# One decoder layer on one core: three strands' products issued later, a division moved from VectorE to ScalarE, and x loaded ahead of the first weights

## The chip, the cores and the metric

The kernel runs on one core of a Trainium2 chip. The metric is the device time of one execution in microseconds (us). TensorE is called PE, VectorE DVE, ScalarE ACT, GpSimd POOL; SP is SyncE, which here only issues DMAs. PEld is the loading of weights into TensorE.

## The reference, cut to what matters

One layer over 256 tokens of width 1024, batch 1, in float32: a token mixer, a mixture of 32 experts, and a per-layer embedding, each followed by a layer norm.

```
proj = h @ w_in                       # 1024 x 10768: operands of all branches and three gates
y_a = gdn_branch(...) @ w_o_gdn       # gated delta rule, chunks, 8 heads of 128
y_b = lru_branch(...) @ w_o_lru       # conv, gated linear recurrence, GeLU gate
y_c = swa_branch(...) @ w_o_swa       # window attention, softmax with a sink
mix = (g_a * y_a + g_b * y_b + g_c * y_c) @ w_out
x = layer_norm(2**0.25 * x + mix)
x = layer_norm(2**0.25 * x + moe(x))  # top 4 of 32: x @ w_gu[e], SwiGLU, @ w_down[e]
x = layer_norm(2**0.25 * x + sigmoid(x Wg) * (p Wp))
```

Two details matter here. The delta rule needs `g = -exp(a_log) * softplus(a + dt_bias)`, its running sum, and the inverse of a triangular 64x64 matrix per head and chunk. The attention needs `probs = pexp / (sum(pexp) + exp(sink - m))`.

## The kernel before, in words

The program has two parts. `mixer` (to about 453 us of the profiled execution) does the token mixer and the router; `moe` then streams 12 MB of weights for each of the 32 experts.

In `mixer`, PE's work is a list of units. A column unit is 24 products of 128x256 (L367), a wide unit 12 products of 128x512 (L377). Each unit needs one 512 KB piece of weights. `load` (L416) has SP fetch it into one of four buffers `w`; `split` casts it on ACT into a high part HI (L423) and subtracts on DVE (L426) and POOL (L428) into a low part LO; HI and LO have three places each, and a piece is split two units ahead of its use. `rows_by` and `column` then multiply high by high, high by low and low by high.

Beside the units run strands: Python generators that `run` steps once a unit, after the unit's products are issued. A `yield` in a strand puts what follows behind the next unit's products on every engine. So the number of yields between an operation and the product that reads it sets how much other PE work lies between them. Each engine takes its instructions in the order in which they were issued and waits for each in turn. Strands that the change touches:

- `softplus` (L278 to L296): a chain of small DVE operations. `parameters` uses it for the recurrence, `evac_ab` for the decay g. After it `evac_ab` multiplies by -exp(a_log) (L597), yields, and has PE form the running sums (L600 to L602); after another yield ACT copies them out (L604) and the event "G" is set.
- `decays` waits for "G" and then has PE spread the sums over 128 columns (L671), four times.
- `inverse` writes its 16x16 blocks to DRAM and back in another layout (L751, L756), yields twice, transposes on DVE (L760) and then runs bursts of 32x32 products on PE: L765 (64 of them), L774 and L777 (64 each).
- `attend`, four times: scores and maximum (L1000 to L1013), exponentials with their sums on ACT (L1017, L1018), sum and reciprocal on DVE (L1022, L1023), the division as a multiplication on DVE (L1025, L1026, eight operations), transposes on PE (L1041), the product with the values (L1053).
- `bias_parts` loads b_gu in twelve pieces of 64 KB through POOL's DMA queue (L234) and splits each into three parts on ACT and POOL (L240, L242, L244).

At the start SP issues the first piece of w_in, then x in four pieces, then more weights; ACT and DVE split the first piece, PE turns x (L271), and units begin.

In `moe` SP loads the experts' weights into ten buffers of 2 MB in a ring; a load waits until PE has done with the buffer.

Of the kernel before, what the change touches and what calls it, by code (L numbers as in the profile page):

```python
# [14 lines left out]
ALU = mybir.AluOpType  # L15
# [5 lines left out]
P = 128  # L21
# [90 lines left out]
def mixer(mx, tc, nc, a, xs, rt, dram, cst, ones, el):  # L112
# [38 lines left out]
    def bank(i):  # L151
        return lambda: pg.tile([P, 512], F32, name="pg", tag=f"pg{i}", bufs=1)
# [25 lines left out]
    def wait(*names):  # L178
        while not all(n in events for n in names):
            yield  # L180
# [10 lines left out]


    warm = mp.tile([P, 1], F32, name="warm")
    pool.memset(warm, 0.0)
    act.dma_start(cst[:, 0:P], a["cst"][:, 0:P])
    act.activation(warm, warm, AF.Sigmoid)
# [28 lines left out]
    def bias_parts():  # L225
        yield from wait("late", "lru")
        raw_b = mp.tile([96, 512], F32, name="rawb")
        bsrc = a["b_gu"][0].rearrange("(g e) (q c) -> g (e q) c", g=4, q=4)
        dve.tensor_add(rt.pick, ident[:96, 0:32], ident[:96, 32:64])
        dve.tensor_add(rt.pick, rt.pick, ident[:96, 64:96])  # L230
        yield
        for g_ in range(4):
            for n in range(3):
                pool.dma_start(raw_b[32 * n:32 * n + 32], bsrc[g_])  # L234
            yield
            yield
            v = rt.bias[:, g_]
            for whole, rows in ((slice(0, 96), (slice(0, 96),)), (slice(64, 96), (slice(32, 64), slice(64, 96)))):
                for r in rows:
                    act.copy(v[r], raw_b[r])  # L240
                yield
                pool.tensor_tensor(out=raw_b[whole], in0=raw_b[whole], in1=v[whole], op=ALU.subtract)  # L242
                yield
            act.copy(v[64:96], raw_b[64:96])  # L244

    pool.memset(ones, 1.0)
    mhalf = mpa.tile([P, 16], F32, name="mhalf")
    pool.memset(mhalf, -0.5)
    upper = mpa.tile([P, 1], F32, name="upper")
# [26 lines left out]
    def softplus(dst, src, n, neg):  # L276

        e = m2.tile([P, n], F32, name="spe", tag="spe")  # L278
        s = m2.tile([P, n], F32, name="sps", tag="sps")
        q = m2.tile([P, n], F32, name="spq", tag="spq")  # L280
        act.activation(e, src, AF.Abs)
        act.activation(e, e, AF.Exp, scale=-1.0)
        yield
        dve.tensor_scalar(s, e, 2.0, None, op0=ALU.add)
        dve.reciprocal(s, s)
        dve.tensor_mul(s, s, e)
        dve.tensor_mul(q, s, s)
        dve.tensor_scalar(e, q, 1.0 / 17, None, op0=ALU.mult)
        yield
        for c in (15, 13, 11, 9, 7, 5, 3):  # L290
            dve.scalar_tensor_tensor(e, e, 1.0 / c, q, ALU.add, ALU.mult)
            if c in (13, 9, 5):
                yield
        dve.scalar_tensor_tensor(e, e, 1.0, s, ALU.add, ALU.mult)
        dve.tensor_scalar(q, src, -1.0 if neg else 1.0, 0.0, op0=ALU.mult, op1=ALU.max)
        dve.scalar_tensor_tensor(dst, e, 2.0, q, ALU.mult, ALU.add)  # L296
# [114 lines left out]
    def load(n):  # L411
        if n < len(order):
            i = order[n][0]
            raw[i] = wp.tile([P, KD * P], F32, name="w", tag="w")
            src = pieces[i][0]
            sync.dma_start(raw[i].rearrange("p (k c) -> p k c", k=src.shape[1]), src)  # L416
# [161 lines left out]
    def evac_ab(ps):  # L578
        abr = m2.tile([16, T], F32, name="abr", tag="sq")
        act.copy(abr, ps[:16])  # L580
        yield
        p2 = yield from banks.take()
        for t in range(2):
            pe.transpose(p2[:, t * 16:(t + 1) * 16], abr[:, t * P:(t + 1) * P], ident[:16, :16])
        yield
        act.copy(ab, p2[:, :32].rearrange("p (t c) -> p t c", t=2))
        banks.done(p2)
        for t in range(2):
            dve.tensor_add(kd[:, t], ab[:, t, 0:H], dtb)
            act.activation(beta[:, t], ab[:, t, H:16], AF.Tanh, scale=0.5)  # L590
        yield
        dve.tensor_scalar(beta, beta, 0.5, 0.5, op0=ALU.mult, op1=ALU.add)
        yield from softplus(flat(g), flat(kd), 16, False)
        act.activation(alog, alog, AF.Exp)
        yield
        for t in range(2):
            dve.scalar_tensor_tensor(g[:, t], g[:, t], -1.0, alog, ALU.mult, ALU.mult)  # L597
        yield
        p2 = yield from banks.take()
        pe.matmul(p2[:, 0:16], cen, flat(g), start=True, stop=True)  # L600
        pe.matmul(p2[:, 16:24], highh, g[:, 0], start=True, stop=True)
        pe.matmul(p2[:, 24:32], lowh, g[:, 1], start=True, stop=True)  # L602
        yield
        act.copy(gcc, p2[:, :32])  # L604
        banks.done(p2)
        dve.tensor_scalar(nG, Gf, -1.0, None, op0=ALU.mult)
        dve.tensor_add(eG[:, 1], Gf[:, 1], c1)
        dve.tensor_sub(eG[:, 0], gl0, Gf[:, 0])
        dve.tensor_add(eq, Gf[:, 1], c1)
        act.activation(eG, eG, AF.Exp)  # L610
        act.activation(eq, eq, AF.Exp)
        events.add("G")
# [46 lines left out]
    def decays():  # L659

        yield from wait("G")
        dts = []
        for t in range(2):
            dt_ = yield from probs.take()
            dts.append(dt_)
            d8 = dt_.rearrange("p a c -> p (a c)")[:, :8 * P].rearrange("p (h c) -> p h c", h=8)
            for h4 in range(2):
                ps = yield from banks.take()
                for i in range(4):
                    h = 4 * h4 + i  # L670
                    pe.matmul(ps[:, i * P:(i + 1) * P], Gf[:, t, h:h + 1].to_broadcast([P, P]), ident, start=True, stop=True)  # L671
                yield
                for i in range(4):
                    h = 4 * h4 + i
                    dve.scalar_tensor_tensor(d8[:, h], ps[:, i * P:(i + 1) * P], nG[:, t, h:h + 1], cmask, ALU.add, ALU.add)
                banks.done(ps)
                yield
                act.activation(d8[:, 4 * h4:4 * h4 + 4], d8[:, 4 * h4:4 * h4 + 4], AF.Exp)
        yield from wait("k", "q", "xc")
        M["PM"] = PM = big("E7", [P, 16, P])  # L680
        M["AT"] = AT = big("AT", [P, 16, P])
        prev = None
        for t in range(2):
            for h2 in range(5 if t else 4):
                cur = None
                if h2 < 4:
                    b_ = yield from banks.take()
                    cur = (t, h2, b_)
                    for ii in range(2):
                        h = 2 * h2 + ii  # L690
                        pe.matmul(cur[2][:, ii * T:(ii + 1) * T], KQ[:, h, 0, t * P:(t + 1) * P],
                                  KQ[:, h, :, t * P:(t + 1) * P], start=True, stop=True)
                if prev:
                    tt, hh2, ps = prev
                    for ii in range(2):
                        h = 2 * hh2 + ii
                        d = dts[tt].rearrange("p a c -> p (a c)")[:, h * P:(h + 1) * P]
                        dve.scalar_tensor_tensor(PM[:, tt * H + h], ps[:, ii * T:ii * T + P], brr[:, tt, h:h + 1], d, ALU.mult, ALU.mult)
                        dve.scalar_tensor_tensor(AT[:, tt * H + h], ps[:, ii * T + P:(ii + 1) * T], rk[:, tt, h:h + 1], d, ALU.mult, ALU.mult)
                    banks.done(ps)  # L700
                prev = cur
                if h2 % 2:
                    yield
        for d in dts:
            probs.done(d)
        events.add("PM")

    def inverse():
# [45 lines left out]
        for b in range(8):  # L754
            c = slice(16 * (b % 2), 16 * (b % 2) + 16)
            sync.dma_start(T0[16 * b:16 * b + 16, :, c], td[b].rearrange("s i c -> i s c"))  # L756
        yield
        yield
        view = lambda ps, s: ps.rearrange("p (s c) -> p s c", s=s)
# [221 lines left out]
    def attend(gq, qT):  # L981
# [40 lines left out]
        dve.tensor_add(sm, sm, es)  # L1022
        dve.reciprocal(sm, sm)  # L1023
        for hh in range(4):
            dve.tensor_scalar(pr3[:, hh, 0:P], pr3[:, hh, 0:P], sm[:, 0, hh:hh + 1], None, op0=ALU.mult)  # L1025
            dve.tensor_scalar(pr3[:, hh, P:384], pr3[:, hh, P:384], sm[:, 1, hh:hh + 1], None, op0=ALU.mult)  # L1026
            if hh == 1:
                yield
        yield
# [265 lines left out]
                       (second(0, 2, 3), ((0, 1),)), (second(1, 0, 1), ()), (second(1, 2, 3), ((1, 1),))):  # L1295
        units.append(out_unit(work, done))

    load(0)
    for i in range(4):
        sync.dma_start(xs[:, :, i * 256:(i + 1) * 256], xsrc[:, :, i * 256:(i + 1) * 256])  # L1300
    load(1)
    load(2)
    sync.dma_start(wg[:, 0], a["rg_w_a"][0].rearrange("h i j -> i h j"))
    sync.dma_start(wg[:, 1], a["rg_w_x"][0].rearrange("h i j -> i h j"))
    load(3)
    split(order[0][0])
    for _ in transpose_x():
        pass
    par = parameters()
    next(par)  # L1310
    spawn(par)
# [507 lines left out]
```

## Time and profile before

| | |
|---|---|
| median of 3 runs | 1422.58 us (1421.93 to 1425.25) |
| the profiled execution | 1420.59 us, of which the profile's span is 1418.8 us |
| mean granted TensorE clock | 0.985 of full speed |
| PE busy | 1343.1 us, 95% (7720 products, 7721 weight loads) |
| DVE, ACT, POOL busy | 591.8, 372.4, 247.0 us |
| DMA over the span | 481.66 MB, 339 GB/s |
| DMA packets that carry instructions (queue q8) | 62, together 1.02 MB |

The span is the time from the first to the last instruction. A busy share is an average over two stages with different limits, so stages are read one by one below. "Granted clock" is the share of TensorE's full clock that was granted; of its two levels 1.0 is 2.4 GHz and 0.5 is 1.2 GHz.

### The profile page before, as it was taken

The numbers are of one execution on the slowest core, as the hardware profiler recorded it, in microseconds if no ns is written. First come the engines' busy times: TensorE is split into PE (matmuls) and PEld (weight loads), VectorE is DVE, ScalarE is ACT, GpSimd is POOL, SyncE is SP. The second block draws the span as 40 slices with busy tenths as digits, with TensorE's granted clock in tenths as the row PEclk, the third lists the DMA queues.
The fourth block names the chain that finished last, engine by engine and source line by source line (L and its number), as shares of the span: only waits on it lengthen the run. The fifth ranks groups of instructions, "written<-read, shape, count | busy, mean of one in ns | idle before, by whom it ended". The sixth has DMA issues, their size and how long they took to land. (4 is left out here: it accounts for less than half of the span.)

```text
span 1418.8 us, 19330 instructions
## 1 busy us (share of the span) xinstructions
PE 1343.1 (95%) x7720; PEld 748.0 (53%) x7721; DVE 591.8 (42%) x1245; ACT 372.4 (26%) x743; POOL 247.0 (17%) x217
## 2 busy tenths in 40 slices
PE   8999989999999999999999999999999999989987
PEld 7989967888887334334333333333333333333326
DVE  6398985865565133223222222222223222222238
ACT  6767464644551111111111110111111100111122
POOL 5554864434561000000000000000000000000000
PEclk9999999999998999999999999999999999999998
DMA  9755455345888999999999999999999999999970
GB/s 264 215 137 138 133 180 168 113 135 181 307 303 339 367 427 430 428 428 426 428 429 428 428 426 429 430 428 428 426 429 430 428 427 428 429 428 428 428 296 30
DMA packets 122133, 481.66 MB, mean 339 GB/s; under 512 B 11340, under 2 KB 69340, under 8 KB 88632
## 3 DMA queue, kind: packets, MB, share of 16 engines
q1 hardware_dynamic: 120440, 477.16, 84.4%
q0 software_dynamic: 848, 1.86, 0.4%
q10 hardware_dynamic: 752, 1.38, 0.3%
q8 instruction: 62, 1.02, 0.3%
q14 instruction: 31, 0.25, 0.0%
HBM read 478.78 MB, written 3.42 MB: 340 GB/s over the span
## 5 line engine op out<-in xcount | busy, mean ns | idle before, releaser
L1485 PE MATMUL gu<-w,xe 128*64 128x512 f32 x1168 | 262.9, 598 | 6.6 <-DMA w<-in_w_gu_dram 6.6
L1485 PE MATMUL gu<-F,xe 128*64 128x512 f32 x880 | 199.2, 596 | 4.8 <-DMA F<-in_w_gu_dram 4.8
L428 POOL TENSOR_TENSOR LO<-w,HI 128x384 fp32r<-128x384 f32 (+1 forms) x113 | 168.4, 1491 | 165.9 <-ACT HI L423 154.6
L1485 PEld LDWEIGHTS gu<-w,xe 128*64 128x64 f32 x1168 | 81.7, 137 | 164.8 <-issue 144.1
L426 DVE TENSOR_TENSOR LO<-w,HI 128x640 fp32r<-128x640 f32 (+1 forms) x113 | 117.1, 1038 | 83.5 <-ACT HI L423 81.8
L1503 DVE TENSOR_SCALAR gc<-gu 128x256 f32<-128x256 f32 x64 | 26.9, 421 | 266.9 <-PE gu L1485 266.9
L1416 POOL DMA_DIRECT2D pt<-in_p_dram x1 | 0.8, 777 | 789.2 <-DVE lc L1507 789.2
L423 ACT CAST HI<-w 128x1024 fp32r<-128x1024 f32 x113 | 118.0, 1044 | 59.2 <-PE pjt L377 36.6
L1520 PE MATMUL dn<-w,hT 128*64 128x512 f32 x560 | 130.0, 607 | 2.0 <-ACT hT L1513 2.0
L1556 DVE TENSOR_TENSOR Y<-Y,cb 128x512 f32<-128x512 f32 x124 | 79.5, 682 | 116.3 <-PE cb L1545 116.3
L367 PE MATMUL pjt<-xh,HI 128*128 128x256 f32 x424 | 124.7, 294 | 0.0
L1485 PEld LDWEIGHTS gu<-F,xe 128*64 128x64 f32 x880 | 60.2, 136 | 119.0 <-issue 104.9
L367 PE MATMUL pjt<-xh,LO 128*128 128x256 f32 x424 | 120.5, 284 | 1.3 <-DVE LO L426 1.3
L367 PE MATMUL pjt<-xl,HI 128*128 128x256 f32 x424 | 120.1, 283 | 0.0
L1520 PE MATMUL dn<-F,hT 128*64 128x512 f32 x464 | 106.0, 598 | 0.0
L1504 ACT ACTIVATE sg<-gc 128x256 f32<-128x256 f32 x64 | 26.8, 419 | 286.4 <-DVE gc L1503 286.4
L1448 PE MATMUL gat<-oh,xs 128*128 128x128 f32 x512 | 76.2, 294 | 24.7 <-DVE oh L1456 19.9
L1448 PEld LDWEIGHTS gat<-oh,xs 128*128 128x128 f32 x512 | 64.4, 197 | 44.4 <-issue 27.7
L367 PEld LDWEIGHTS pjt<-xh,HI 128*128 128x128 f32 x424 | 81.5, 192 | 1.8 <-issue 1.1
L367 PEld LDWEIGHTS pjt<-xh,LO 128*128 128x128 f32 x424 | 81.3, 192 | 2.0 <-DVE LO L426 1.9
L367 PEld LDWEIGHTS pjt<-xl,HI 128*128 128x128 f32 x424 | 81.5, 192 | 0.3
L1493 DVE TENSOR_TENSOR gt<-gwt,gt 128x256 fp32r<-128x256 f32 x32 | 13.6, 424 | 152.2 <-ACT gt L1492 152.2
(404 smaller groups left out, 1713.2 us busy)
## 6 DMA issues: line engine op xcount, KB each, us to landing
w<-in_w_gu_dram SPq DMA_DIRECT2D x73, 2048.0 KB, 29.2
F<-in_w_gu_dram SPq DMA_DIRECT2D x51, 2048.0 KB, 29.4
w<-in_w_down_dram SPq DMA_DIRECT2D x70, 1024.0 KB, 19.3
F<-in_w_down_dram SPq DMA_DIRECT2D x58, 1024.0 KB, 21.0
w<-in_w_in_dram SPq DMA_DIRECT2D x85, 512.0 KB, 3.8
F<-in_w_gu_dram SPq DMA_DIRECT2D x8, 1024.0 KB, 6.8
w<-in_w_o_lru_dram SPq DMA_DIRECT2D x8, 512.0 KB, 4.7
w<-in_w_o_swa_dram SPq DMA_DIRECT2D x8, 512.0 KB, 3.8
```

Source lines behind the costliest of these rows:

```text
L367: pe.matmul(ps, hl[l][:, k * P:(k + 1) * P], b[r][:, k], start=k == 0 and n == 0, stop=k == KD - 1 and n == 2)
L423: act.copy(hi, s)
L426: dve.tensor_sub(lo[:, 0:n], s[:, 0:n], hi[:, 0:n].bitcast(F32))
L428: pool.tensor_tensor(out=lo[:, n:], in0=s[:, n:], in1=hi[:, n:].bitcast(F32), op=ALU.subtract)
L1416: pool.dma_start(pt, a["p"][0, 0].rearrange("(t p) c -> p t c", p=P))
L1448: pe.matmul(ps[:, kk], xs[:, t, k * P:(k + 1) * P], oh[:, t], start=t == 0, stop=t == 1)
L1485: pe.matmul(gu[64 * j:64 * j + 64, b], xe[:, k], w[:, j * D + b * 512:j * D + (b + 1) * 512], start=False, stop=k == KD - 1)
L1493: dve.tensor_sub(gt[:, 1], ps, gt[:, 0].bitcast(F32))
L1503: dve.tensor_scalar(gc[:, c], guv[:, c, 0], 7.0, None, op0=ALU.min)
L1504: act.activation(sg[:, c], gc[:, c], AF.Sigmoid, scale=1.702)
L1520: pe.matmul(dn[64 * jj:64 * jj + 64], hT[:, 2 * hf + kk, j * 64:j * 64 + 64], w[:, kk, jj * 512:(jj + 1) * 512], start=hf == j == kk == 0, ...
L1556: dve.tensor_add(y, y, pss[jj])
```

## The change

It edits six places; line numbers behind the first edit grow by one to eight.

1. `ones` is set first on POOL; x is loaded ahead of the first piece of weights, its turning on PE is issued ahead of the first split, and PE gets twelve 128x128 products of `ones` with itself, into a PSUM bank that nobody reads.
2. The twelve loads of b_gu go through SP's queue.
3. `softplus` yields once inside its chain of seven steps instead of three times.
4. One yield more ahead of the running sums in `evac_ab`, and one in `decays` behind "G".
5. Two yields more in `inverse`, between the loads of T0 and the transpose.
6. The softmax division runs on ACT.

```diff
     warm = mp.tile([P, 1], F32, name="warm")
+    pool.memset(ones, 1.0)
     pool.memset(warm, 0.0)
...
             for n in range(3):
-                pool.dma_start(raw_b[32 * n:32 * n + 32], bsrc[g_])
+                sync.dma_start(raw_b[32 * n:32 * n + 32], bsrc[g_])
...
-    pool.memset(ones, 1.0)
...
             dve.scalar_tensor_tensor(e, e, 1.0 / c, q, ALU.add, ALU.mult)
-            if c in (13, 9, 5):
+            if c == 9:
                 yield
...
             dve.scalar_tensor_tensor(g[:, t], g[:, t], -1.0, alog, ALU.mult, ALU.mult)
+        yield
         yield
         p2 = yield from banks.take()
         pe.matmul(p2[:, 0:16], cen, flat(g), start=True, stop=True)
...
         yield from wait("G")
+        yield
         dts = []
...
             sync.dma_start(T0[16 * b:16 * b + 16, :, c], td[b].rearrange("s i c -> i s c"))
         yield
         yield
+        yield
+        yield
...
         for hh in range(4):
-            dve.tensor_scalar(pr3[:, hh, 0:P], pr3[:, hh, 0:P], sm[:, 0, hh:hh + 1], None, op0=ALU.mult)
-            dve.tensor_scalar(pr3[:, hh, P:384], pr3[:, hh, P:384], sm[:, 1, hh:hh + 1], None, op0=ALU.mult)
+            act.mul(pr3[:, hh, 0:P], pr3[:, hh, 0:P], sm[:, 0, hh:hh + 1])
+            act.mul(pr3[:, hh, P:384], pr3[:, hh, P:384], sm[:, 1, hh:hh + 1])
...
-    load(0)
     for i in range(4):
         sync.dma_start(xs[:, :, i * 256:(i + 1) * 256], xsrc[:, :, i * 256:(i + 1) * 256])
+    load(0)
+
+    ps = bank(4)()
+    for _ in range(12):
+        pe.matmul(ps[:, 0:P], ones, ones, start=True, stop=True)
     load(1)
...
-    split(order[0][0])
     for _ in transpose_x():
         pass
+    split(order[0][0])
```

In PE's order the units stay the same 117 in the same order. The running sums (L600 to L602) stand behind unit 27 instead of unit 28; the first spreading (L671) stays behind unit 29, the other three too. L765 moves from behind unit 55 to behind unit 57, L774 with L777 from 57 to 59, and the rest of `inverse` by two units; its end, which the next strand waits for, is met at the same unit 71 as before.

The chain of softplus for the decay g on DVE (seven steps L291 on spe, then L294). Before, its third pair of steps and the last one:

```order
L291 SCALAR_TENSOR_TENSOR spe<-spe,spq 128x16 x2
L462 SCALAR_TENSOR_TENSOR cv<-pjt,cw,cv 128x255
L462 SCALAR_TENSOR_TENSOR cv<-pjt,cw,cv 128x254
L462 SCALAR_TENSOR_TENSOR cv<-pjt,cw,cv 128x253
L426 TENSOR_TENSOR LO<-w,HI 128x640
L630 SCALAR_TENSOR_TENSOR KQ<-th,cv 128x256
L291 SCALAR_TENSOR_TENSOR spe<-spe,spq 128x16
L294 SCALAR_TENSOR_TENSOR spe<-spe,sps 128x16
```

Two pairs stand ahead of these rows, a unit apart each; behind them come the multiplication L597 one unit later and L600 on PE another unit later. Now, all seven steps:

```order
L291 SCALAR_TENSOR_TENSOR spe<-spe,spq 128x16 x4
L462 SCALAR_TENSOR_TENSOR cv<-pjt,cw,cv 128x255
L462 SCALAR_TENSOR_TENSOR cv<-pjt,cw,cv 128x254
L462 SCALAR_TENSOR_TENSOR cv<-pjt,cw,cv 128x253
L426 TENSOR_TENSOR LO<-w,HI 128x256
L631 SCALAR_TENSOR_TENSOR KQ<-th,cv 128x256
L291 SCALAR_TENSOR_TENSOR spe<-spe,spq 128x16 x3
L294 SCALAR_TENSOR_TENSOR spe<-spe,sps 128x16
```

The seven steps stood in four units and stand in two; L597 comes two units earlier and PE's sums one, so two units lie between them instead of one.

POOL, behind the memsets of `inverse` (U and T1 in RV). Before:

```order
L736 MEMSET U 128x2048
L737 MEMSET RV 64x1024
L234 DMA rawb<-in_b_gu_dram 32x512 x3
L428 TENSOR_TENSOR LO<-w,HI 128x384 x3
L242 TENSOR_TENSOR rawb<-rawb,bias 96x512
```

And now:

```order
L738 MEMSET U 128x2048
L739 MEMSET RV 64x1024
L428 TENSOR_TENSOR LO<-w,HI 128x384 x3
L243 TENSOR_TENSOR rawb<-rawb,bias 96x512
```

The three DMA issues left POOL's order; on SP they stand behind the bias of the second `attend` and one piece of weights.

ACT, at the first `attend`'s division (F holds the probabilities, st the sums). Before:

```order
L536 ACTIVATE TG<-pjt 128x512 x2
L423 CAST HI<-w 128x1024
L240 CAST bias<-rawb 32x512 x2
L1017 ACTIVATE F_97,st<-F_97,st 128x128
L1018 ACTIVATE F_97,st<-F_97,st 128x256
L423 CAST HI<-w 128x1024
```

And now:

```order
L536 ACTIVATE TG<-pjt 128x512 x2
L423 CAST HI<-w 128x1024
L241 CAST bias<-rawb 32x512 x2
L1029 ACTIVATE F_97<-F_97,st 128x128
L1030 ACTIVATE F_97<-F_97,st 128x256
L1029 ACTIVATE F_97<-F_97,st 128x128
L1030 ACTIVATE F_97<-F_97,st 128x256
L1021 ACTIVATE F_97,st<-F_97,st 128x128
L1022 ACTIVATE F_97,st<-F_97,st 128x256
L423 CAST HI<-w 128x1024
```

Four multiplications that need DVE's reciprocal now stand on ACT ahead of the cast of a piece of weights; the other four stand behind it, ahead of the next cast.

## Rows read from the trace of the kernel before

**Rows 1.** Busy time by stretch: core length, engines, granted clock, DMA share, GB/s.

```profile
458.00:462.00 4.00, 4.00 (x23) 1.69 (x20) 0.00 (x0) 0.37 (x1) 0.00 (x0) 1.00 0.00 0
500.00:540.00 40.00, 38.44 (x200) 16.10 (x198) 13.68 (x29) 5.32 (x14) 0.00 (x0) 1.00 1.01 430
...
1300.00:1340.00 40.00, 38.74 (x176) 14.36 (x172) 11.54 (x26) 5.94 (x14) 0.00 (x0) 1.00 1.01 430
```

**Rows 2.** Waits of PE over the whole span: for whom, us in total, times, longest.

```profile
PE pg L777 <- issue: 2.9, 1, 2.9
...
PE pg L671 <- ACT gcc L604: 2.0, 1, 2.0
...
PE pjt L377 <- POOL LO L428: 1.8, 1, 1.8
PE pg L600 <- DVE sc L597: 1.7, 1, 1.7
PE pjt L377 <- DVE LO L426: 1.5, 1, 1.5
PE pjt L377 <- DVE cv L462: 1.4, 1, 1.4
PE pjt L367 <- DVE LO L426: 1.3, 3, 0.6
```

**Rows 3.** Busy time by stretch, around three drops of the granted clock.

```profile
84.00:112.00 28.00, 23.22 (x185) 21.97 (x183) 25.86 (x57) 17.02 (x36) 13.21 (x11) 1.00 0.46 123
112.00:116.00 4.00, 3.85 (x19) 3.85 (x20) 2.39 (x8) 1.90 (x8) 1.90 (x2) 0.57 0.52 134
190.00:194.00 4.00, 4.00 (x11) 3.11 (x11) 2.16 (x7) 3.68 (x13) 1.89 (x2) 0.58 0.74 234
224.00:232.00 8.00, 6.21 (x126) 4.06 (x127) 1.95 (x5) 2.27 (x4) 1.48 (x4) 0.57 0.33 94
```

**Rows 4.** Instructions in order of time, 186 to 192 us: start, length, [idle before <- releaser].

```profile
187.12 1.58 POOL L234 DMA_DIRECT2D rawb<-in_b_gu_dram  x3
...
190.32 0.62 ACT L240 CAST bias<-rawb 96x512 bf16<-96x512 f32 x1 [5.75 <-DMA rawb<-in_b_gu_dram]
```

**Rows 5.** Groups of instructions, 160 to 300 us: busy us, mean ns.

```profile
L1018 ACT ACTIVATE F<-F,st 128x256 f32<-128x256 f32 x16 | 7.9, 494 | 0.0
...
L1026 DVE TENSOR_SCALAR F<-F,st 128x256 f32<-128x256 f32 x16 | 7.1, 444 | 0.0
L1025 DVE TENSOR_SCALAR F<-F,st 128x128 f32<-128x128 f32 x16 | 6.7, 422 | 0.1
```

**Rows 6.** Instructions in order of time around the first division, 196 to 210 us.

```profile
196.54 1.25 ACT L240 CAST bias<-rawb 32x512 bf16<-32x512 f32 x2
...
198.71 1.03 ACT L423 CAST HI<-w 128x1024 fp32r<-128x1024 f32 x1
...
199.98 0.21 DVE L1023 RECIPROCAL st<-st 128x8 f32<-128x8 f32 x1
```

**Rows 7.** Instructions in order of time, 208 to 240 us: in the 32x32 bursts.

```profile
225.79 1.64 PE L777 MATMUL pg<-RV,KT 32*32 32x32 f32 x105 [2.92 <-issue]
```

**Rows 8.** DMA queues from 222.9 to 224.2 us: packets, MB, share of 16 engines.

```profile
q8 instruction: 1, 0.02, 4.6%
```

**Rows 9.** Instructions in order of time, 0 to 45 us: the start.

```profile
5.75 0.83 DVE L426 TENSOR_TENSOR LO<-w,HI 128x640 fp32r<-128x640 f32 x1 [5.64 <-ACT HI L423]
...
7.21 2.72 PE L271 MATMUL pg<-cst,xs 128*128 128x128 f32 x12 [0.51 <-DMA xs<-in_x_dram]
...
10.11 0.28 PE L367 MATMUL pjt<-xh,LO 128*128 128x256 f32 x1
...
10.47 0.28 PE L367 MATMUL pjt<-xh,LO 128*128 128x256 f32 x1
```

**Rows 10.** The loads of x: issue ns, first and last issue us; time to landing.

```profile
L1300 SPq DMA_DIRECT2D xs<-in_x_dram x4: 462/469/573, 1.3 to 2.9; - x4
...
DMA to landing us min/median/max: 4.2/5.2/5.5
```

## The prediction, made before the run

> **What bounds the kernel now.** I read the busy times by stretch first, since the mean hides two stages. From 500 us to past 1340 us the DMA engines are busy all the time (share 1.01, 430 GB/s) while PE has about 1.5 us idle in 40: the experts' weights set the pace [rows 1]. Just ahead of it, from 458 to 462 us, nothing is transferred: the ring of ten buffers is full, and the stream goes on when PE frees the first [rows 1]. So a microsecond gained by PE before 458 us starts the stream a microsecond earlier, and the rest follows one for one; what an engine saves in the expert stage would be worth nothing. The change touches the token mixer alone.
>
> In the mixer PE sets the pace, apart from its waits. The list of PE's waits names them: 2.0 us at L671, 1.7 at L600, 1.8 for POOL's low part, 1.5 and 1.3 for DVE's, 1.4 for a convolution on DVE, and 2.9 in the middle of L777 with no releaser ("issue") [rows 2]. Then the clock: after three of these places the granted clock stands at its 1.2 GHz level for a while. The work lost is (1 minus granted clock) times the stretch: 0.43 x 4 = 1.7 us at 112, 0.42 x 4 = 1.7 at 190, 0.43 x 8 = 3.4 at 224 [rows 3]. Ahead of each PE had idled, 2.0, 1.8 and 2.9 us [rows 2]; behind the gaps of 1.5 and 1.4 us no such stretch lies in these rows.
>
> **Running sums (84 to 116 us).** Lost now: 1.7 at L600, 2.0 at L671, 1.7 by the clock, 1.3 by DVE's low parts, in all 6.7. L600 waits for L597 on DVE, which is issued one unit ahead; the change makes that two units, a unit being 24 products at (10.47 - 10.11) / 3 = 0.12 us [rows 9], 2.9 us, more than the 1.7 that is missing. L671 stands in the same step as the copy that it reads; now the copy is one unit earlier and L671 where it was, so 2.9 us stand against 2.0. By the yields alone 1.7 + 2.0 + 1.7 = 5.4 us go. What is late next is DVE: it is busy 25.9 of 28 us and 2.4 of the next 4 [rows 3], so it has 2.1 + 1.6 = 3.7 us of air there, and the stretch can't get shorter by more, unless some of DVE's work slides behind 116 us. Ends 3.7 and 5.4; I take 4.2, near the lower, as DVE's queue is what these strands wait in. The shorter softplus has the same fourteen DVE operations, so it costs nothing but their place.
>
> **POOL's queue (184 to 190 us).** The three issues of b_gu take 1.58 us of POOL, from 187.12 to 188.7 [rows 4], and the low part that PE waits for stands right behind them in POOL's order. Without them it starts 1.6 us earlier and 1.6 of the wait of 1.8 goes. The remaining 0.2 should leave the clock up: 1.7 more. ACT stands 5.75 us for that load [rows 4]; on SP it no longer stands behind POOL's memsets, so that stall should go; I count nothing for it, as PE hardly waits on ACT here. On SP the twelve issues stand ahead of weights that are fetched three pieces ahead, so they cost nothing; if that cover were gone, the same 1.6 us a group of three. From the second group on, SP must also wait until ACT has copied the buffer (L244), and all weights queue behind that; ACT does it right behind the cast of the unit, and SP's next load waits for that piece's low part anyway.
>
> **The division (196 to 290 us).** DVE loses 7.1 + 6.7 = 13.8 us of work. ACT gains 32 operations; the trace does not show them, but exponentials of the wider shape, with a sum, take 0.494 us [rows 5], an upper end for both shapes (15.8 us in all); a lower one is what DVE loses halved, 6.9. I take 0.3 and 0.4, 11.2 us, that is 1.4 us for each half of a division. ACT is not the bound (busy 17 of 28 us in one of its fuller stretches [rows 3]), but its queue is in order. At the first division ACT is done with its casts at 196.54 + 1.25 = 197.8, and the reciprocal ends at 200.2 [rows 6]: ACT would stand 2.4 us, multiply for 1.4, and only then reach the cast of weights that ran at 198.71. That cast would be 3.7 us late, about what lay between its end and its use. So of DVE's 1.5 us wait [rows 2], which came from these multiplications ahead of the low part, I count 0.3 as won (ends -2.4 and 1.5: one unhidden stand of ACT, or all of it). Further on, the 1.4 us wait for the convolution [rows 2] has four DVE multiplications ahead of it, 2 x (0.42 + 0.44) = 1.7 at their means; I count 0.9 (ends -0.5, as ACT's four stand ahead of the same convolution's first step, and 1.4).
>
> **The 32x32 bursts (212 to 232 us).** The two added yields give the loads of T0 more time, but no wait of PE on them is listed, so they win nothing there. What is lost, 2.9 us idle and 3.4 by the clock, falls in L777. There, in the middle of 64 small products, PE stood 2.92 us until 225.79 with no releaser [rows 7], and within that gap one packet of 0.02 MB passes in the queue that carries instructions [rows 8]. I read it as PE running out of instructions. L774 and L777 stay neighbours, so the gap stays; I count 0.5 us for the wide unit that now follows and may bring the clock back sooner. Ends: 6.3, if the gap goes; -6.3, if L765, which falls elsewhere in the instruction stream, gets one too. The Trainium skill says in "Runtime: NRT & Kernel Launch", section "Instruction fetch mechanics", that 16 KiB blocks of instructions are fetched ahead and that the fetch is hidden because the sequencer dispatches slower than the blocks arrive. By that page the gap has another cause, two more units would cure it, and the term would be 6.3 instead of 0.5; the packet inside the gap speaks against it.
>
> **The start.** Now the first product that needs the low part runs at 10.11 us [rows 9]; x, 1 MB behind 0.5 MB of weights, has landed by 2.9 + 5.5 = 8.4 [rows 10]. After the change the weights come last in the same 1.5 MB and land where x did, at 8.4. Then cast (1.03 [rows 6]) and low part (0.83 [rows 9]) follow, 10.3: 0.2 later than now. The twelve unread products are 24 passes (a float32 product runs as two) at 2.72 / 12 = 0.23 us [rows 9], 5.4 us from about 1.2 us on, so they end before 7 us, and x is turned in 1.8 to 3.6 us while the weights come. What they win is hidden behind the weights. Between x and the first cast PE then idles 2 us or more, and gaps of 1.8 to 2.9 us led to the low clock three times: 1.7 us at perhaps one in two, 0.8. In all 1.0 us lost; ends 2.5 lost and 0.8 won (weights landing at 7.5, as the third piece of x might).
>
> **Sum.** 4.2 + (1.6 + 1.7) + 0.3 + 0.9 + 0.5 - 1.0 = 8.2 us. Against the profiled execution, 1420.6 (span 1418.8 and 1.8 around it), that is 1412.4. The profiled execution is 2.0 us below the median of the runs, so for the median 1422.6 - 8.2 = 1414.4 us. One measurement of this kernel tells about 0.3%, 4.3 us, from no change.
>
> **The rivals.**
> *DVE binds (0.20).* The waits move from L600 and L671 to DVE's low parts, since DVE is 92% busy in that stretch [rows 3], and the clock falls anyway. Then 84 to 116 us yields 2.1, POOL's queue 1.6, the start costs 1.0 and the rest nothing: 2.7 won, 1419.9. For it: the three waits on L426 there [rows 2]. Against: PE never waited there for as long as a unit.
> *The gap in L777 goes too (0.12).* 8.2 + 6.3 - 0.5 = 14.0 won: 1408.6. For it: the order around it changes. Against: [rows 8]; the burst is as dense as before.
> *A second gap, at L765 (0.10).* 8.2 - 6.3 = 1.9 won: 1420.7. For it: 64 products issue there as densely. Against: today only L777 has such a wait [rows 2], and a single burst is half as long.
> *ACT stands for the reciprocal (0.08), slower.* Each of the four divisions makes ACT stand 2.4 us ahead of a cast; where that cast is then late, PE waits 2.4 and loses 1.7 by the clock. At two of them this takes back 3.3 + 0.3 + 0.9 (POOL's queue and the division) and adds 8.2: 8.2 - 4.5 - 8.2 = 4.5 lost, 1427.1. It decides when the stand and the multiplications together exceed the some 4 us between a cast and its use. For it: [rows 6]. Against: ACT's 5.75 us stall is gone, so its queue is less full, and DVE is freed of the work that made its reciprocals late.
>
> **How the numbers follow.** The forecast holds 0.50. Faster by over 0.3% (below 1418.3): nearly all of the forecast (0.48), all of the gone gap (0.12), a quarter of DVE binding (0.05): 0.65. Slower by over 0.3%: 0.07 from ACT and 0.01 from the others: 0.08. The rest, 0.27, is within. The likeliest case alone spans 1410 to 1418. The range to hold 8 in 10 takes in DVE binding, most of the second gap and the edge of the gone gap: 1408 to 1421.5.
>
> **What the profile of the changed kernel would show.** Right: L600 and L671 gone from PE's waits and the clock at 1.0 through 112 to 116 us; no wait on POOL near 190 and the clock up there; the 2.9 us "issue" wait still in L777; the stretch without transfers, the expert stage and the end all earlier by the same amount; the first product with a low part at 10 to 10.5 us. Wrong: new waits on ACT's HI at the divisions, a low clock in the first 14 us for longer than I counted, a second "issue" wait behind L765, or an expert stage that ends later than the mixer's gain says.

## The result, and the profile after

The changed kernel takes 1432.12 us (median of 5 runs, 1431.02 to 1435.11) against 1421.93 for the kernel before in the same rounds: a ratio of 1.0077, 95% interval 1.0062 to 1.0092. It is slower by 10 us; 1414.4 was forecast. Its profiled span is 1428.8 us against 1418.8, so the traces show the same 10.0 us.

The first question is which stage lost it. The expert stage only passes it on: the stretch without transfers that lay at 458 to 462 us before [rows 1] lies at 468 to 472 now. Busy time by stretch in the changed kernel (the columns are those of [rows 1]):

```profile
458.00:462.00 4.00, 2.87 (x14) 2.74 (x13) 1.35 (x9) 0.32 (x1) 0.00 (x0) 0.50 1.02 430
...
468.00:472.00 4.00, 4.00 (x22) 1.59 (x18) 0.00 (x0) 0.37 (x1) 0.00 (x0) 1.00 0.00 1
```

Up to 168 us the two kernels are level (the first product of scores starts at 168.5 us after the change, at 168.6 before). The loss lies between 184 and 300 us. The same view of the kernel before, and then of the changed one:

```profile
184.00:200.00 16.00, 13.69 (x51) 10.48 (x52) 13.28 (x52) 10.19 (x28) 10.50 (x12) 0.89 0.53 171
200.00:232.00 32.00, 27.61 (x495) 20.86 (x495) 22.79 (x46) 15.82 (x27) 15.80 (x17) 0.89 0.63 186
232.00:300.00 68.00, 66.48 (x617) 57.76 (x618) 52.81 (x119) 42.57 (x91) 31.27 (x23) 1.00 0.43 123
```

```profile
184.00:200.00 16.00, 12.53 (x47) 9.47 (x47) 13.83 (x51) 8.60 (x24) 8.48 (x8) 0.89 0.57 176
200.00:232.00 32.00, 27.69 (x255) 21.10 (x254) 13.41 (x34) 20.54 (x43) 16.45 (x11) 0.95 0.62 177
232.00:300.00 68.00, 60.44 (x810) 52.42 (x809) 46.25 (x88) 44.77 (x103) 26.51 (x17) 0.92 0.38 107
```

Take PE's idle time (length minus busy) and add (1 minus granted clock) times the length. Before: idle 2.3 + 4.4 + 1.5 = 8.2, clock 0.11 x 16 + 0.11 x 32 = 5.3, in all 13.5 us. After: idle 3.5 + 4.3 + 7.6 = 15.3, clock 1.8 + 1.6 + 5.4 = 8.8, in all 24.1. The difference, 10.6, is about the 10.0 that the span grew by.

PE's waits name the places (changed kernel; for whom, us in total, times, longest). These lines answer to [rows 2]:

```profile
PE pjt L377 <- ACT TG L536: 7.7, 2, 4.3
PE pg L781 <- issue: 4.2, 1, 4.2
PE pjt L367 <- DVE LO L426: 2.3, 5, 0.6
...
PE pjt L367 <- POOL LO L428: 1.0, 1, 1.0
...
PE pg L639 <- ACT sq L635: 0.7, 1, 0.7
```

The waits at the running sums are gone, as forecast. New and largest are two waits for ACT's TG, the evacuation of a gate's bank, 3.4 us at 194.6 and 4.3 at 212.3. The second one, read in order of time on the four engines (start, length, [idle before <- releaser]):

```profile
207.26 1.03 ACT L423 CAST HI<-w 128x1024 fp32r<-128x1024 f32 x1
...
208.32 0.83 DVE L426 TENSOR_TENSOR LO<-w,HI 128x640 fp32r<-128x640 f32 x1 [1.76 <-ACT HI L423]
208.37 1.63 POOL L428 TENSOR_TENSOR LO<-w,HI 128x384 fp32r<-128x384 f32 x1 [0.93 <-ACT HI L423]
209.06 0.96 DVE L1026 TENSOR_TENSOR st<-st 128x8 f32<-128x8 f32 x1
210.06 0.20 DVE L1027 RECIPROCAL st<-st 128x8 f32<-128x8 f32 x1
210.30 0.40 ACT L1029 ACTIVATE F<-F,st 128x128 f32<-128x128 f32 x1 [2.00 <-DVE st L1027]
...
211.69 1.05 ACT L536 ACTIVATE TG<-pjt 128x512 f32<-128x512 f32 x2
...
212.32 1.22 PE L377 MATMUL pjt<-HI,F 128*128 128x512 f32 x2 [4.31 <-ACT TG L536]
```

ACT is done with its cast at 208.3. Next in its queue is the division, which needs DVE's reciprocal. DVE was itself waiting for that cast, does the low part first, then the sum and the reciprocal. So ACT stands 2.0 us, multiplies for 1.4, and only then empties the bank that PE has needed since 208.0. Behind it the clock falls (208 to 216 us: 0.79, against 1.00 before).

### The profile page after: what moved, and what is told of

Same layout as the page of the kernel before. It is cut to its first block, busy times and chain, and to the rows that moved or that the text cites. A ratio compares the mean times of both kernels' runs of the same rounds, so it can differ in the third digit from the quotient of the medians.

```text
span 1428.8 us, 19379 instructions
## 1 busy us (share of the span) xinstructions
PE 1352.6 (95%) x7744; PEld 754.1 (53%) x7745; DVE 582.2 (41%) x1213; ACT 383.2 (27%) x775; POOL 244.3 (17%) x205
## 3 DMA queue, kind: packets, MB, share of 16 engines
q0 software_dynamic: 464, 1.07, 0.2%
## 5 line engine op out<-in xcount | busy, mean ns | idle before, releaser
L428 POOL TENSOR_TENSOR LO<-w,HI 128x384 fp32r<-128x384 f32 (+1 forms) x113 | 171.5, 1519 | 184.5 <-ACT HI L423 174.4
L1528 PEld LDWEIGHTS dn<-w,hT 128*64 128x64 f32 x560 | 37.8, 139 | 73.0 <-issue 61.9
```

What stands on the lines that cost most here:

```text
L428: pool.tensor_tensor(out=lo[:, n:], in0=s[:, n:], in1=hi[:, n:].bitcast(F32), op=ALU.subtract)
L1528: pe.matmul(dn[64 * jj:64 * jj + 64], hT[:, 2 * hf + kk, j * 64:j * 64 + 64], w[:, kk, jj * 512:(jj + 1) * 512], start=hf == j == kk == 0, ...
```

## The experiments

Times are medians of 5 to 12 runs; ratios are to the kernel before in the same rounds, whose medians were 1420.9 to 1421.7 us. "Us back" is the distance to the changed kernel's 1432.12, which was measured in other rounds, so it is good to about a microsecond.

### What the division costs

**e1: the changed kernel, division back on DVE.**

```diff
-            act.mul(pr3[:, hh, 0:P], pr3[:, hh, 0:P], sm[:, 0, hh:hh + 1])
+            dve.tensor_scalar(pr3[:, hh, 0:P], pr3[:, hh, 0:P], sm[:, 0, hh:hh + 1], None, op0=ALU.mult)
```

(and the same for the second line)

> The changed kernel with the softmax division back on DVE, all else kept. Theory (ACT, whose queue is in order, stands for the reciprocal at the divisions, and the evacuations of TG that PE needs stand behind it): the wait of 4.3 us on TG near 208 us goes with the 1.7 us of clock behind it, and most of the 2.0 + 0.9 + 0.5 us of waits near 273 to 294 us with 1.7 us of clock: some 8 us, 1424 (1421 to 1426). Rival (DVE's queue is late because of the inverse and the loads of b_gu, and the division only stands in the way): PE waits as long, on DVE instead of ACT: 1430 to 1434.

1424.19 us (ratio 1.0019, 1.0010 to 1.0028): 7.9 us back. The wait at 212 us is gone, the one at 194.7 (3.4 us) stays: it isn't the division's.

**e2: the kernel before, division on ACT alone** (the same edit the other way).

> The kernel before with the division on ACT as the only edit. Theory (ACT stands for the reciprocal): a wait of 2.4 to 4.3 us on TG or HI after one or two divisions, each with 1.7 us of clock: 1426 to 1431. Rival (the division is harmless by itself and only together with the later inverse does ACT stand): 1420 to 1422.

1432.22 us (1.0082, 1.0068 to 1.0096), a microsecond above the range of the theory, and the rival is out. One edit alone loses 11.3 us, about as much as all six. PE's waits in it:

```profile
PE pjt L377 <- ACT TG L536: 4.8, 2, 4.3
PE pjt L377 <- DVE cv L462: 2.9, 1, 2.9
...
PE pjt L377 <- ACT HI L423: 1.3, 1, 1.3
```

The wait for the convolution, which I had hoped to shorten, has doubled from 1.4 [rows 2]. The other 1.3 us, for the high part HI, is at the first division. Busy time by stretch in e2:

```profile
184.00:200.00 16.00, 13.63 (x53) 10.10 (x50) 13.29 (x52) 8.51 (x23) 10.88 (x11) 0.89 0.53 179
200.00:232.00 32.00, 24.95 (x372) 18.75 (x370) 12.93 (x28) 21.12 (x45) 17.50 (x15) 0.89 0.54 163
232.00:300.00 68.00, 63.56 (x676) 52.92 (x677) 45.20 (x95) 45.01 (x104) 28.78 (x23) 0.92 0.36 108
```

Idle and clock come to 13.9 + 10.7 = 24.6 us here, against 13.5 before.

**e5: the changed kernel, the multiplications still on ACT but one unit behind the reciprocal.**

```diff
         dve.reciprocal(sm, sm)
+        yield
         for hh in range(4):
...
         yield
-        yield
         PT = yield from PTs.take()
```

> The changed kernel with the eight multiplications of each division still on ACT, but issued one unit after the reciprocal (a yield is moved from behind them to between). Theory (what costs is that ACT stands for a reciprocal that DVE reaches late, with TG and HI queued behind): the stands of about 2 us go, the wait of 4.3 us near 208 us shrinks by 2 to 4.3 and its clock loss of 1.7 goes: 1425 to 1429. Rival (what costs is the work of 1.4 us per half on ACT, in an already full queue): 1430 to 1433.

1423.84 us (1.0018, 1.0009 to 1.0027): 8.3 us back, as much as by e1 and a little more than expected, although ACT does the same work. The second division in order of time:

```profile
206.71 1.03 ACT L423 CAST HI<-w 128x1024 fp32r<-128x1024 f32 x1
207.65 1.07 ACT L536 ACTIVATE TG<-pjt 128x512 f32<-128x512 f32 x2
...
208.52 0.99 DVE L1026 TENSOR_TENSOR st<-st 128x8 f32<-128x8 f32 x1
...
209.54 0.20 DVE L1027 RECIPROCAL st<-st 128x8 f32<-128x8 f32 x1
...
210.07 0.40 ACT L1030 ACTIVATE F<-F,st 128x128 f32<-128x128 f32 x1
```

DVE's reciprocal is ready at 209.7, hardly earlier than before; but TG now stands ahead of the multiplications and goes at once. The cost was the place in the queue, ahead of TG, and not the amount of work on ACT.

### The bursts and the inverse

**e3: the changed kernel without the inverse's two yields.**

```diff
         yield
         yield
-        yield
-        yield
         view = lambda ps, s: ps.rearrange("p (s c) -> p s c", s=s)
```

> The changed kernel without the two added yields of the inverse. Theory (the stand of ACT): the wait on TG near 208 us stays, since the inverse's yields stand behind it in the program: 1430 to 1434. Rival (the two units by which the inverse is late cost the time: the wait at its 64x64 products, 0.9 us, and the larger issue gap, 4.2 instead of 2.9): 1432 - 0.9 - 1.3 and some clock: 1427 to 1430.

1427.01 us (1.0042, 1.0028 to 1.0055): 5.1 us back, the rival's side. TG's waits stay (7.5 us in all), the issue gap is 2.7 instead of 4.2, and the wait for the convolution is 2.9 instead of 0.5, as in e2.

**e4: the changed kernel, one wide unit between the two neighbouring bursts.**

```diff
                 pe.matmul(view(b1, 16)[q, s], U0[q, s], Xn[q, s], start=True, stop=True)
+        yield
         for s in range(16):
             for q in qs:
                 pe.matmul(view(b2, 16)[q, s], Xn[q, s], U0[q, s], start=True, stop=True)
```

> The changed kernel with one yield, thus one wide unit of PE, between the two groups of 64 products of 32x32 that now stand neighbours (T0's and U0's refinement). Theory (PE runs out of instructions in so dense a burst; with a wide unit between, the next block has time to come): the issue gap of 4.2 us goes, and the clock behind it (0.10 x 4 + 0.50 x 4 + 0.25 x 4 = 3.4 us): 1424.5 (1423 to 1427). Rival (the gap has another cause that is bound to the second group, such as what it waits for): the gap stays before the second group, 1431 to 1434.

1425.86 us (1.0030, 1.0018 to 1.0041): 6.3 us back; the gap is 0.9 instead of 4.2. This kernel's runs spread most, from 1421.6 to 1428.9 us, and the trace is of one of 1428.5, so the 6.3 is the least certain of these numbers.

**b1: the same split alone on the kernel before.**

> The kernel before with one wide unit between the two neighbouring groups of 32x32 products as the only edit. Theory (PE runs out of instructions in the dense burst): of the gap of 2.9 us about 2 goes, as the split left 0.9 in the changed kernel, and the clock's 3.4 behind it: 1421.3 - 5.4 = 1416 (1414.5 to 1417.5). Rival (the gap is bound to something else that the changed kernel's order removed): 1420 to 1422.

1417.90 us (0.9971, 0.9960 to 0.9982). 3.8 us won, a little less than expected: 1.2 us of the gap remain, while the clock stays at 1.00 from 224 to 232 us, where it was 0.57 [rows 3].

**o1: the inverse's two yields alone on the kernel before.**

> The kernel before with the inverse's two added yields as the only edit. Theory (the burst of 32x32 products falls otherwise against the blocks of instructions, and its gap is 4.2 instead of 2.9 us, with a longer stretch at the low clock): 1421.6 + 3.9 = 1425.5 (1424 to 1427). Rival (the two units cost only where ACT stands for the division): 1421 to 1422.5.

1422.81 us (1.0010, 1.0001 to 1.0019): 1.4 us lost, nearer to the rival.

**o5: both, the yields and the split.**

> The kernel before with the inverse's two added yields and one wide unit between the two groups of 32x32 products. Theory (the yields cost by the gap in the burst alone): as the split alone, 1417.9 (1417 to 1419.5). Rival (they cost because the inverse is late for its readers): 1417.9 + 3.9 = 1421.8 (1420.5 to 1423).

1417.31 us (0.9974, 0.9965 to 0.9983), the same as the split alone. So with the burst split the yields cost nothing, and being two units late harms no reader. The gap in four kernels (before it is [rows 7]): the changed one, o1, b1 and o5.

```profile
241.56 0.90 PE L781 MATMUL pg<-RV,KT 32*32 32x32 f32 x49 [4.23 <-issue]
```

```profile
237.79 0.55 PE L779 MATMUL pg<-RV,KT 32*32 32x32 f32 x25 [4.68 <-issue]
```

```profile
230.57 0.28 PE L778 MATMUL pg<-RV,KT 32*32 32x32 f32 x9 [1.19 <-issue]
```

```profile
236.50 0.56 PE L780 MATMUL pg<-RV,KT 32*32 32x32 f32 x41 [1.05 <-issue]
```

### The other edits, alone on the kernel before

**e6: the running sums** (`if c == 9`, and the two yields; as in the change's diff).

> The kernel before with the running sums' edits alone (one yield in the softplus instead of three, one more ahead of the product with cen, one more ahead of the decays). By the prediction's term 4.2 us: 1416.7, with 3.7 to 5.4: 1415.5 to 1417.2. By the trace of the changed kernel (PE busy in 84 to 130 us 43.05 instead of 41.07, and 1.6 us of clock back, but 1.0 and 0.7 us of new waits by 143 us): 3.6 - 1.7 = 1.9: 1419.

1421.70 us (1.0003, 0.9993 to 1.0013): nothing won, below both expectations. PE's waits in it:

```profile
PE pjt L377 <- POOL LO L428: 2.7, 1, 2.7
...
PE pjt L377 <- ACT TG L536: 2.2, 1, 2.2
...
PE pjt L367 <- DVE LO L426: 1.9, 4, 0.6
...
PE pjt L367 <- POOL LO L428: 1.0, 1, 1.0
...
PE pg L639 <- ACT sq L635: 0.7, 1, 0.7
```

The waits at the sums and the low clock are gone, but the last three lines are new or longer, and the first two have grown from 1.8 [rows 2] and 0.5.

**e7: b_gu through SP** (`pool.dma_start` becomes `sync.dma_start`).

> The kernel before with the twelve loads of b_gu issued by SP instead of POOL as the only edit. By the prediction's term 1.6 + 1.7 = 3.3 us: 1417.6. By the trace of the changed kernel (no wait on POOL near 188, but 3.4 us on TG at 191 and the clock low behind it, since ACT's exponential waits for DVE's row maxima): nothing won or lost, 1420 to 1422.

1422.02 us (1.0010, 0.9997 to 1.0022): nothing won. POOL's wait falls from 1.8 [rows 2] to 0.7, and PE then stands 3.9 us for TG. What precedes that, on DVE, POOL and ACT:

```profile
189.71 0.23 DVE L743 TENSOR_TENSOR F<-KT 128x63 f32<-128x63 f32 x1
...
190.09 1.03 POOL L428 TENSOR_TENSOR LO<-w,HI 128x384 fp32r<-128x384 f32 x1 [0.49 <-ACT HI L423]
...
190.23 0.96 DVE L743 TENSOR_TENSOR F<-KT 128x64 f32<-128x64 f32 x1
...
191.06 1.16 POOL L242 TENSOR_TENSOR rawb<-rawb,bias 96x512 f32<-96x512 f32 x1
191.23 1.07 DVE L745 TENSOR_TENSOR KT<-KT,F 128x64 f32<-128x64 f32 x1
...
194.19 0.21 ACT L1015 ACTIVATE st<-st 128x8 f32<-128x8 f32 x1 [3.29 <-DVE st L1013]
...
195.18 1.06 ACT L536 ACTIVATE TG<-pjt 128x512 f32<-128x512 f32 x2
```

ACT stands 3.3 us for DVE's row maxima ahead of the exponentials, and TG is queued behind. It is the fault of the division again, at another operation. DVE was late for a reason that the edit made: its chain of small operations ran beside POOL's DMA issues before and runs beside POOL's tensor operations now, where two of them take 0.96 and 1.07 us instead of 0.23.

**b2: b_gu through SP, and the exponentials one unit later.**

```diff
         dve.tensor_sub(es, skb, mxv)
         yield
+        yield
         act.activation(es, es, AF.Exp)
```

(one of the two yields behind the division is taken out)

> The kernel before with the loads of b_gu on SP and the exponentials of the softmax issued one unit later, the unit taken from behind the division. Theory (on SP the loads free POOL, but ACT then stands for DVE's row maxima with TG queued behind, which takes the gain back): the wait of 3.9 us on TG near 192 us goes or falls below 1.5, and with it the clock's 1.7: 1422 - 2.4 - 1.7 = 1418 (1416 to 1419.5). Rival (DVE is simply late there, and PE stands for its low parts instead): 1421 to 1423.

1418.47 us (0.9977, 0.9965 to 0.9988): 3.2 us won, as many as were predicted for b_gu, now that TG doesn't stand behind DVE. The wait on TG is gone and the clock is 1.00 in 184 to 200 us. But the later exponentials were not timed without b_gu's move, and in this trace PE's wait for DVE's low part is also shorter (0.6 us, 1.5 before) and the one for the convolution is not listed (1.4 before). So how much of the 3.2 us each of the two edits wins is not shown.

**e8: the start** (as in the change's diff).

> The kernel before with the new start alone (x ahead of the first weights, the unread products, ones written first). By the prediction's term 1.0 us lost: 1421.9 (1420.1 to 1423.4). Rival (the unread products keep the clock up and x being there early is worth more): 1418 to 1420.

1422.41 us (1.0007, 0.9997 to 1.0017): 1.1 us above, within what can't be told from nothing.

**b4: start, b_gu and running sums together** (the changed kernel without division and inverse).

> The changed kernel without its division and its inverse edit, thus the kernel before with the start, b_gu on SP and the running sums. If the inverse's two units cost what they cost beside the division (5.1 us, 1432.1 - 1427.0): 1424.2 - 5.1 = 1419. If that cost was the meeting with ACT's stands: 1422 to 1425, as without the division alone.

1420.30 us (0.9994, 0.9985 to 1.0003): what the four edits that don't harm are worth together, nothing, with TG's wait of 3.2 us still in place.

### A kernel that beats both

**b3: running sums, b_gu on SP, exponentials one unit later, burst split;** division, inverse and start as before.

> The kernel before with the running sums' edits, b_gu on SP, the exponentials one unit later and the split of the burst; division on DVE, the inverse and the start as before. If the two stalls that took the gains back are named rightly, the gains add: 1421.3 - 2 to 4 (running sums) - 3 (b_gu with the later exponentials) - 5.4 (split) = 1409 to 1411. Rival (one of them only uncovers DVE at the next place): 1414 to 1417.

1413.87 us (0.9945, 0.9932 to 0.9959), 7.8 us won, between the expectations.

```profile
184.00:200.00 16.00, 13.31 (x58) 10.37 (x56) 15.01 (x46) 12.34 (x34) 11.88 (x11) 1.00 0.62 200
200.00:232.00 32.00, 30.47 (x515) 23.11 (x516) 22.35 (x59) 16.44 (x27) 13.10 (x10) 1.00 0.63 186
232.00:300.00 68.00, 67.01 (x628) 58.56 (x627) 57.39 (x114) 41.82 (x91) 29.75 (x21) 1.00 0.43 135
```

Idle 2.7 + 1.5 + 1.0 = 5.2 us and no clock lost, where the kernel before loses 13.5 in these stretches.

**o8: the same without the running sums.**

> The combined kernel (1413.9) without the running sums' edits: b_gu on SP, the exponentials one unit later, the burst split. If the running sums are worth the predicted 4.2 us once ACT's stand for the row maxima is gone: 1418 (1417.5 to 1419). If most of it is lost to DVE's and POOL's low parts already by 168 us, where 1.2 us of it were left in the combined kernel's trace: 1415 (1414.3 to 1415.8).

1414.71 us (0.9948, 0.9933 to 0.9963): the running sums are worth 0.8 us here, with overlapping intervals; 4.2 is excluded.

## Why the prediction was wrong

**The division: the step that failed.** The text let ACT stand 2.4 us and multiply for 1.4, and the trace of the division alone shows this (2.42 us in e2, 1.4 per half). The failing sentence is "That cast would be 3.7 us late, about what lay between its end and its use". It looked at the cast of weights and at the first division alone; there PE waited 1.3 us for the cast (e2). It did not ask what else is queued on ACT: the evacuation TG, which PE needs in the very next unit, and which has no slack. At the second division TG stood behind the stand and the multiplications, and PE waited 4.3 us, with the clock behind it. Counted at +0.3 and +0.9, the edit alone is worth -11.3 (e2): PE's waits grew by 4.3 us for TG, 1.5 for the convolution and 1.3 for HI, the 1.5 for DVE's low part went as hoped, and the clock took 5.4 more between 184 and 300 us, in all 11.0. The rival "ACT stands for the reciprocal", with 0.08 as its chance and 8.2 us as its price, was right that ACT stands and that PE pays for it with the clock; it put PE's wait at the casts, and most of it was at TG. e5 shows that it was what stood ahead of TG. Against it I had set that ACT's 5.75 us stall for b_gu was gone. It was not (4.0 us are left of it), and it lies ahead of the first division, where it could not have decided what stands behind the second.

**POOL's queue.** The wait on POOL shrank as forecast, though by 1.1 us instead of 1.6 (1.8 to 0.7 in e7), but the 3.3 us did not come. The text passed over ACT with "PE hardly waits on ACT here". PE hardly waited because it was late itself. Coming earlier, it meets ACT standing for the row maxima: PE goes on at 194.6 after the change, at 195.2 before. With the exponentials moved too, b2 wins 3.2 us.

**The running sums.** The places and the clock came as forecast: clock 1.00 in 112 to 116 us (0.57 before, [rows 3]). The size was wrong: 4.2 taken, none found alone (e6) and 0.8 in company (b3 against o8). New waits of 0.6, 1.0 and 0.7 us follow up to 143 us in e6, on DVE's and POOL's low parts and on ACT. The first product of scores, at the same unit, starts at 168.0 us in e6 against 168.6. The forecast's rival "DVE binds" comes nearer, though POOL and ACT bind beside DVE; some of what was won by 116 us is not accounted for by listed waits. Part of what the edit was to win is also not lost in every run: in e8 and o8, with these lines as before, the clock falls already behind L600, and PE then stands 0.4 us at L671 instead of 2.0.

**The bursts.** "The gap stays" was right, the term of +0.5 was not: alone the yields lost 1.4 us (o1), in company 3.9 (b4 to e1) and 5.1 (e3). With the burst split they lose nothing (o5), so alone their cost is the gap's: 4.2 to 4.7 us in the unsplit kernels with the yields, one gap of 2.7 to 3.2 us or two that come to 3.4 or 3.5 (e8, b4) without. Why it costs more beside the other edits than alone is open: the profiled spans of e1 and b4 differ by only 1.4 us. The rival's second gap, behind L765, came in e1 only (1.2 us at L769).

That PE runs out of instructions there is now better supported, though it stays an inference. In e8 the only difference ahead of the burst is the new start, whose twelve unread products pass PE as 24, as the 64 of a burst pass as 128; the gap moved ahead by about as many passes, from behind the 23rd of L777 (105 were left [rows 7]) to the end of L774, and a second one appears 128 passes further on:

```profile
224.31 0.18 PE L774 MATMUL pg<-KT,RV 32*32 32x32 f32 x1 [1.24 <-issue]
...
224.37 1.23 PE L777 MATMUL pg<-RV,KT 32*32 32x32 f32 x123
227.76 0.21 PE L777 MATMUL pg<-RV,KT 32*32 32x32 f32 x2 [2.17 <-issue]
```

The changed kernel has the same start, and against o1 its gap has moved by 24 as well (49 left of L781, 25 in o1). The packet that the prediction saw inside the gap need not lie inside it: in e8, packets of the instruction queue pass at 221.72 and 225.34 us, ahead of the two gaps.

```profile
q8 instruction: 1, 0.02, 23.3%
```

```profile
q8 instruction: 1, 0.02, 26.1%
```

(DMA queues of e8 in 221.6 to 221.9 and 225.2 to 225.5 us.) What holds in every trace is the distance: PE goes on 2.2 to 3.0 us after such a packet (223.58 and 225.79 us before, 239.24 and 241.56 after, 221.72 and 224.31 in e8). So the place hangs on how many instructions lie ahead, and a wide unit between the bursts takes most of the gap away. The Trainium skill, "Runtime: NRT & Kernel Launch", section "Instruction fetch mechanics", calls the crossing of a 16 KiB block mostly hidden. If these gaps are such crossings, the traces differ for these bursts, with gaps of up to 4.7 us (o1), and the measurement decides.

**The start.** Forecast 1.0 us lost, measured 1.1 lost without being told from nothing; the agreement is luck, as the parts were otherwise. The first product with a low part comes at 11.24 us instead of 10.11 [rows 9] (10.3 was forecast). The forecast let the cast follow the landing of the weights; on ACT it now stands behind the casts of x:

```profile
7.33 2.05 ACT L272 CAST xh<-pg 128x512 fp32r<-128x512 f32 x4 [4.58 <-PE pg L271]
...
9.25 2.12 ACT L423 CAST HI<-w 128x1024 fp32r<-128x1024 f32 x2
```

The clock stays up in the changed kernel (PE's wait there is 1.7 us), in e1, e3 and e8. In e4, e5 and b4, with the same start, it is at 0.50 from 12 to 14 us behind a wait of 1.9 us, and 1.7 us of work is lost. So the forecast's "one in two" for the clock was about right, and the medians hold a mix.

**From the mixer to the end.** One for one, as forecast: the stretch without transfers moved by 10 us and so did the end.

## What to carry to other kernels

Before an operation is moved to an engine with an in-order queue, list everything that is queued behind its new place until the operand is ready, and give each its own deadline: the tightest one, here the emptying of a PSUM bank, sets the price, not the operation's duration or the engine's busy share. Leave a step of the schedule between the engine that makes the operand and the one that reads it. And where a wait is removed, look for what else the waiting engine would have met at that time; here two stands side by side cost as much as the longer one, and removing one won nothing while the other stayed (e7).

## What the runs showed of the hardware

- A short DVE operation on SBUF alone that starts while POOL is in a tensor operation ended with it: 128x63 took 0.23 us alone, 128x64 took 0.96 us started 0.14 us into POOL's 1.03 (e7), and the division's sum of 128x8 took 0.96 beside L428. DVE's L1009, which reads a PSUM bank, was not held: 0.42 us at 190.94, inside POOL's 190.73 to 191.73 (changed kernel). POOL's 128x384 took about 1.0 us, and 1.6 where it started just behind the start of DVE's low part. The Trainium skill, "Trainium Architecture — The Big Picture", section "What this means for kernel authors", says that DVE and GpSimd share a port by an exclusive lock; the traces agree. So POOL's DMA issues, which I counted as a cost, were also 1.58 us [rows 4] in which DVE's short chain ran undisturbed (0.21 to 0.23 us an operation).
- ACT's multiplications with a column took 0.394 (128x128) and 0.495 us (128x256), as long as the exponentials (0.395 and 0.494), 14.2 us for 32 against the 11.2 that I took.
- A gap in PE's stream of instructions lies within the dense bursts of 32x32 products, and an unrelated edit over 200 us earlier moved it by as many passes as it added (e8). It ended 2.2 to 3.0 us after a packet of the instruction queue in every trace here.
- The granted clock falls behind short idles of PE, but not behind each: in the start it fell behind 1.9 us in e4, e5 and b4 and stayed up behind 1.9 in e1.
